# A hybrid decoder layer on one core: earlier fetch of attention's results, two gates moved back, the last inverse from smaller blocks, and tiles shifted by 64 bytes

## The chip, the cores and the metric

The kernel runs on one core of a Trainium2 chip. The metric is the device time of one execution in microseconds; three executions of the kernel before are given, and a profiled one beside them. All numbers of the profile come from that one execution. Its engines are called as the profile calls them: PE (TensorE, matmuls), PEld (the weight loads of TensorE), DVE (VectorE), ACT (ScalarE), POOL (GpSimd) and SP (SyncE, which issues the DMAs).

## The reference, cut to what matters

One layer works on x of 512 tokens by 1024 channels, in float32:

```python
h = rms_norm(x, norm1_w) * (1 + sc1) + sh1
proj = h @ w_in                     # attention q, k, v | RWKV r, k, v and low-rank inputs | 2 x 1024 gates
y_att = attention_mixer(att_in) @ w_att_out
y_rwkv = rwkv7_mixer(rwkv_in, ...) @ w_rwkv_out
g_att, g_rwkv = split(sigmoid(gate_in + b_gate))
x = x + gt1 * ((g_att * y_att + g_rwkv * y_rwkv) @ w_o)
h = rms_norm(x, norm2_w) * (1 + sc2) + sh2
x = x + gt2 * conv_ffn(h, w_up, conv_w, conv_b, w_down)
out = rms_norm(x, norm_f_w)
```

The RWKV mixer carries a 64 by 64 state in each of 16 heads over the 512 tokens:

```python
state = state * w_t + sa * bb_t + v_t * k_t     # sa = state @ aa_t
y_t = state @ r_t
```

## The kernel before, in words

**Products in two halves.** Every large float32 matrix is split into a rounded high part and the rest (`split_w`, `weights`), and a product is three matmuls: high by high, high by low, low by high. ScalarE makes the high part, VectorE the low one. Raw weights come by DMA into a tile with the tag `raw` (two buffers in the pool `wp`), their halves go to `whi` and `wlo` (two buffers each), and a matmul has 128 rows, 128 columns of weights and 512 moving columns.

**The RWKV part by chunks.** The 512 tokens are cut into 8 chunks of 64. The 16 heads make 8 pairs, and two pairs make a group: 4 groups, numbered 0 to 3. For a pair (`pair`, line 1223 on) the projections k, r and v are made, then decays, the products within a chunk (`gram`, tile `gt`) and transposed operands. For a group (`inverse`, line 1436 on) the triangular 64 by 64 matrices of its 32 heads and chunks are inverted at once. Then `chain` (line 1572 on) goes through the 8 chunks in order, each with a few small matmuls that depend on the chunk before, and it ends with a norm over each head (`norm`), transposes (`ty`, into the PSUM tile `t`), and the multiplication with the group's gates.

**The inverse.** A 64 by 64 block is taken as two 32 by 32 diagonal blocks and one below them. `blocks` copies the diagonal blocks out of `gt` (ScalarE), `turned` transposes them so that VectorE works on 32 partitions' worth of blocks side by side, `scaled` multiplies by the reciprocal norms. The recurrence runs from row 30 down to 0 on VectorE: `two(j)` does two rows with a product (L1512), a sum (L1514) and a correction (L1515); `step(j)` does one of the last three rows (L1504, L1505). `rows` and `rows11` transpose back (L1521, L1526), and TensorE makes the block below the diagonal in two visits, `first_pe` and `second_pe`, which write a PSUM tile with the tag `t`. This tag has one buffer; the group's gate product and the transposes at a chain's end use it too.

**The order of the work.** In the RWKV part each instruction is a task of a planner (`Plan`): engine, estimated time, priority, what it waits for, and what it takes and gives back of counted rooms (a buffer of a tile). The planner simulates the engines with these estimates and writes out one order for each engine. The chip keeps that order: an instruction that waits holds all that come behind it on its engine, and the same holds for the DMA queue on SP. Chains and inverses come first; projections of later pairs, of the 16 branch gates (`early_gate`) and of the attention output (`att_out`) fill TensorE with the lowest priority, in the order in which they are created.

**Gates and the attention product.** The 16 gate projections (8 for attention, m = 0 to 7, and 8 for RWKV) have no place in SBUF while pairs are built. `early_gate(m)` makes one, applies tanh (ScalarE, L1816) and stores it in DRAM. When all tasks that are marked `pre` have ended, the sixteen stores among them, the pairs' pool is closed (`close_pre`, t0); `gates` then loads the first eight gates into the pool `pp2`. When the chains of groups 0 and 2 have ended too (`close_even`, t1), the buffers of the even groups are closed, and then `att_out` runs: it loads attention's results in four parts of 256 KB (`load_part`, tag `ld`), splits each into `ahi` and `alo`, and makes 8 blocks of the attention product (`pa`, 12 matmuls each), each multiplied by its gate. `rwkv_ahead` loads and splits the RWKV results of the first groups (`yhi`, `ylo`) and begins three blocks of the RWKV output product (`pr`) as far as groups 0 to 2 reach. Behind the planned part `early_gates` loads the gates 8 to 15, and `rwkv_out`, `mix_out` (product `o` with W_o), `ffn_first`, `ffn_up` (`u`) and `ffn_down` (`o` again) follow.

**Places in SBUF.** Pools on the left are stacked from the bottom, pools on the right from the top. On the left, from below: `cp` (constants), `wp` (weights), then the stage's own, such as `hp` (h's halves `hhi`, `hlo`), `rp`, `cw`, `gp1`, `ip`, `gp0`, later `wo`, `mp` and `fp`. On the right: `pp` (the pairs), later `pp2`, `attp`, `yp`, then `x1p`, `hp2` (`h2hi`, `h2lo`), `uw` (weights of one block of the up projection) and `op`.

Of the kernel before, what the change touches and what calls it, by code (L numbers as in the profile page):

```python
# [10 lines left out]
F32 = mybir.dt.float32  # L11
F32R = mybir.dt.float32r
AF = mybir.ActivationFunctionType
ALU = mybir.AluOpType
# [114 lines left out]
class Layer:  # L129
# [72 lines left out]
    def consts(self):  # L202
# [17 lines left out]
        self.sel2 = cp.tile([P, 2], F32, name="sel2")  # L220
# [820 lines left out]
    def rwkv(self, tail):  # L1041
# [17 lines left out]
        def half():  # L1059

            self.half = self.ip.tile([P, 2], F32, name="half")
            nc.vector.tensor_reduce(self.half, self.ident.rearrange("p (q s y) -> p s q y", q=4, s=2), axis=AX.XY,
                                    op=ALU.add)
# [26 lines left out]
        self.att_out(t1)  # L1090
# [480 lines left out]

    def chain(self, g):
# [132 lines left out]
        for i in range(2):  # L1705
# [43 lines left out]
            t = pe(1.05, gate, [t, self.sgs], S_, take=("t",), give=("g2",), name="gg")  # L1749
            gt_ = sca(0.6, gate_out, [t], E_, take=("gg",), give=("t",))  # L1750
# [32 lines left out]
    def norm(self, yts, t, deps, T_):  # L1783
# [9 lines left out]
        def var():  # L1793
            d["var"] = cw.tile([P, 4], F32, tag="var", name=self.n("var"))
            nc.vector.tensor_reduce(d["var"], d["sq"], axis=AX.X, op=ALU.add)

        def scale():
            rs = cw.tile([P, 4], F32, tag="rs", name=self.n("rs"))
# [19 lines left out]
    def gates(self, opened):  # L1818
# [10 lines left out]
    def early_gates(self, pool):  # L1829
        self.tr_ = [pool.tile([P, S], F32, name=f"gate{m}", tag=f"gate{m}") for m in range(KD, 2 * KD)]  # L1830
# [16 lines left out]
    def open_late(self, pool, lp):  # L1847

        self.lp = lp
        self.ahi, self.alo = [pool.tile([P, 4, S], F32R, name=x, tag=x) for x in ("ahi", "alo")]  # L1850
        self.yhi, self.ylo = [lp.tile([P, KD, S], F32R, name=x, tag=x) for x in ("yhi", "ylo")]

    def att_out(self, opened):

        nc = self.nc
        parts = [self.load_part(lambda k=k: self.att_d[:, k, :], lambda k=k: self.ahi[:, k, :],
# [348 lines left out]
```

## Time and profile before

| | |
|---|---|
| three executions | 1234.45 us median, 1233.17 to 1236.06 |
| the profiled execution | 1231.72 us, span 1230.0 us |
| mean granted PE clock | 0.984 |
| DMA | 139.41 MB, 113 GB/s over the span |
| group 3's recurrence on DVE, first to last operation | 670.83 to 695.99 us |
| the last early gate's matmul on PE begins | 683.22 us |
| group 3's chain on PE begins | 708.29 us |
| last matmul of group 3's chain begins | 754.85 us |
| the up projection's last stretch and the down projection | 858 to 1103 us, 1106 to 1220 us |

The stage that the change touches lies between 655 and 780 us. The stretches before (attention, the first groups) and behind (from 780 on) keep PE busy throughout, but for some short waits.

How to read the views: a row of the timeline has its start and its length in us, the engine, the line, the operation, the tiles (written tile, arrow, read tiles), the shape, the count, and in brackets the idle time of the engine before it with what ended it. Nearly all matmuls have the line L148, a helper; they are told apart by their tiles: `pg<-hhi,whi` a gate, `pa` the attention product, `pr` the RWKV product, `u<-h2hi` the up projection, `u<-cen,v`, `xy`, `xo` and `u<-xs` a chain, `pe` the inverse's visits, `t<-ident,yt` the transposes behind a chain. A matmul's length is modelled and overlaps the next; how often they start is the measure of their pace. The view of stretches has, for each stretch, its length, the busy time of each engine with the count of instructions that touch it, the granted PE clock (1.00 is full), the share of the DMA engines and GB/s.

### The profile page before, as it was taken

The numbers are of one execution on the slowest core, as the hardware profiler recorded it, in microseconds if no ns is written. First come the engines' busy times: TensorE is split into PE (matmuls) and PEld (weight loads), VectorE is DVE, ScalarE is ACT, GpSimd is POOL, SyncE is SP. The second block draws the span as 40 slices with busy tenths as digits, with TensorE's granted clock in tenths as the row PEclk, the third lists the DMA queues.
The fourth block names the chain that finished last, engine by engine and source line by source line (L and its number), as shares of the span: only waits on it lengthen the run. The fifth ranks groups of instructions, "written<-read, shape, count | busy, mean of one in ns | idle before, by whom it ended". The sixth has DMA issues, their size and how long they took to land.

```text
span 1230.0 us, 18481 instructions
## 1 busy us (share of the span) xinstructions
PE 1179.3 (96%) x7200; PEld 946.1 (77%) x7200; DVE 750.2 (61%) x1266; ACT 542.4 (44%) x1011; POOL 109.2 (9%) x228
## 2 busy tenths in 40 slices
PE   4999999999999999999999599999999999999997
PEld 3788887889778776767786467788888888878886
DVE  5687862431668977846896844764556556652135
ACT  4374521522565474465545443444444444442123
POOL 4000000000000013132103122014000000000001
PEclk9899999999999999999999799999999999999999
DMA  9845872120233342413241525460232323233331
GB/s 316 249 132 166 273 229 66 45 80 18 69 103 94 90 112 74 126 47 98 80 114 43 163 58 178 156 206 18 69 103 86 103 86 102 86 103 103 103 120 68
DMA packets 168902, 139.41 MB, mean 113 GB/s; under 512 B 8849, under 2 KB 150251, under 8 KB 168815
## 3 DMA queue, kind: packets, MB, share of 16 engines
q1 hardware_dynamic: 168671, 137.98, 37.0%
q8 instruction: 56, 0.92, 0.3%
q14 instruction: 31, 0.25, 0.1%
q10 hardware_dynamic: 144, 0.26, 0.1%
HBM read 127.65 MB, written 10.56 MB: 112 GB/s over the span
## 4 chain that ended last, share of the span: by engine, by line
PE 79%; DVE 11%; DMA 6%; ACT 2%; issue 2%; SPq 0%; POOL 0%; POOLq 0%; DVEq 0%; ACTq 0%
PE u L148 22%; PE o L148 13%; PE v L148 7%; PE pg L148 7%; PE qk L148 5%; DMA araw<-in_w_ada_dram 4%; PE k L148 3%; PE r L148 2%; PE pa L148 2%; PE pr L148 2%; PE early L148 2%; PE po L148 2%; PE xy L148 2%; PE pt L151 1%; DVE tt L1514 1%
## 5 line engine op out<-in xcount | busy, mean ns | idle before, releaser
L194 DVE TENSOR_TENSOR wlo<-raw,whi 128x1024 fp32r<-128x1024 f32 x65 | 79.7, 1225 | 146.7 <-ACT whi L193 146.6
L148 PE MATMUL u<-h2lo,whi 128*128 128x512 f32 (+2 forms) x368 | 142.3, 387 | 0.0
L148 PE MATMUL u<-h2hi,whi 128*128 128x512 f32 (+2 forms) x368 | 142.3, 387 | 0.0
L148 PE MATMUL u<-h2hi,wlo 128*128 128x512 f32 (+2 forms) x368 | 142.2, 386 | 0.0
L1136 ACT CAST whi<-raw 128x1024 fp32r<-128x1024 f32 (+2 forms) x73 | 72.5, 994 | 123.7 <-PE qk L148 49.5
L193 ACT CAST whi<-raw 128x1024 fp32r<-128x1024 f32 x65 | 68.2, 1049 | 106.5 <-PE o L148 53.7
L1139 DVE TENSOR_TENSOR wlo<-raw,whi 128x1024 fp32r<-128x1024 f32 (+2 forms) x73 | 83.7, 1149 | 19.1 <-ACT whi L1136 18.8
L148 PEld LDWEIGHTS u<-h2lo,whi 128*128 128x128 f32 x368 | 68.9, 187 | 16.0 <-POOL h2lo L405 0.2
L148 PEld LDWEIGHTS u<-h2hi,wlo 128*128 128x128 f32 x368 | 68.9, 187 | 15.5
L148 PEld LDWEIGHTS u<-h2hi,whi 128*128 128x128 f32 x368 | 68.9, 187 | 15.4
L2028 DVE SCALAR_TENSOR_TENSOR u<-u,cols,u 128x511 f32<-128x511 f32 x88 | 65.7, 747 | 4.3 <-ACT u L2026 2.7
L148 PE MATMUL qk<-hhi,wlo 128*128 128x512 f32 x160 | 64.0, 400 | 0.0
L148 PE MATMUL qk<-hlo,whi 128*128 128x512 f32 x160 | 63.6, 397 | 0.0
L148 PE MATMUL qk<-hhi,whi 128*128 128x512 f32 x160 | 63.5, 397 | 0.0
L148 PE MATMUL o<-whi,fhi 128*128 128x512 f32 x144 | 56.1, 390 | 0.3 <-DVE u L2028 0.3
L148 PE MATMUL o<-wlo,fhi 128*128 128x512 f32 x144 | 56.0, 389 | 0.0
L148 PE MATMUL o<-whi,flo 128*128 128x512 f32 x144 | 56.0, 389 | 0.0
L148 PE MATMUL pg<-hhi,wlo 128*128 128x512 f32 x128 | 51.8, 405 | 0.0
L148 PE MATMUL pg<-hlo,whi 128*128 128x512 f32 x128 | 51.7, 404 | 0.0
L148 PE MATMUL pg<-hhi,whi 128*128 128x512 f32 x128 | 51.7, 404 | 0.0
L810 DVE CUSTOM_DVE_ANT_0 sm<-sc,m 128x256 f32<-128x256 f32 (+1 forms) x64 | 23.9, 404 | 37.6 <-PE sc L148 36.5
L347 DVE SCALAR_TENSOR_TENSOR acc<-araw,cols,acc 128x1024 f32<-128x1024 f32 x28 | 35.8, 1280 | 17.2 <-DMA araw<-in_w_ada_dram 17.1
(414 smaller groups left out, 2778.3 us busy)
## 6 DMA issues: line engine op xcount, KB each, us to landing
raw<-in_w_in_dram SPq DMA_DIRECT2D x62, 512.0 KB
raw<-in_w_up_dram SPq DMA_DIRECT2D x44, 512.0 KB
araw<-in_w_ada_dram SPq DMA_DIRECT2D x32, 512.0 KB
raw<-in_w_down_dram SPq DMA_DIRECT2D x22, 512.0 KB
araw<-in_w_ada_dram SPq DMA_DIRECT2D x32, 256.0 KB
wvraw<-in_w_in_dram SPq DMA_DIRECT2D x20, 256.0 KB
gate_d<-gs SPq DMA_DIRECT2D x16, 256.0 KB
gate<-gate_d SPq DMA_DIRECT2D x16, 256.0 KB
```

The costliest lines, as they stand in the source:

```text
L148: return self.nc.tensor.matmul(out, lhsT, rhs, start=start, stop=stop)
L151: self.nc.tensor.matmul(out, in_, self.ident[: in_.shape[0], : in_.shape[0]], is_transpose=True, start=start, stop=stop,)
L193: self.nc.scalar.copy(hl[0], raw)
L194: (lo_eng or self.nc.vector).tensor_tensor(hl[1], raw, hl[0], op=ALU.subtract)
L347: nc.vector.scalar_tensor_tensor(d["acc"], raw, ck, d["acc"], op0=ALU.mult, op1=ALU.add)
L810: nc.vector.tensor_tensor_reduce(d["sm", h][:, :wd], d["sc"][h][:, :wd], m[:, 256 - wd : 256] if gi == 0 else m[:, :wd], 1.0, 3.0e38, op0= ...
L1136: nc.scalar.copy(d["w"][0], d["raw"])
L1139: nc.vector.tensor_tensor(d["w"][1], d["raw"], d["w"][0], op=ALU.subtract)
L1514: nc.vector.tensor_reduce(t[:, n0:, j - 1 : j + 1], x, axis=AX.X, op=ALU.add)
L2028: nc.vector.scalar_tensor_tensor(u[:, d:], pu[:, : S - d], ch(c), u[:, d:], op0=ALU.mult, op1=ALU.add)
```

## The change

- *Late gates.* The gates m = 6 and 7 are no longer early ones. They are projected behind the other fourteen, and their tanh goes straight into `pp2` when the pairs' pool is closed; they are neither stored nor loaded. The close of the pairs' pool (t0) waits for fourteen stores.
- *Attention's results* are fetched at t0 instead of t1, in two loads of 512 KB into the weights' `raw` tiles instead of four of 256 KB into `ld` tiles. `ahi` and `alo` are eight tiles in a pool opened with `pp2`; the gates 8 to 15 are loaded later into these same tiles.
- *The last inverse* (group 3) is made by `inverse16`: the recurrence runs over 16 by 16 blocks, and TensorE joins them into 32 by 32 blocks in two more visits (`half_pe`), each followed by a copy out of PSUM (`half_out`). The other groups keep `inverse`.
- *Rooms.* A group's gate product takes its room `gg` at the matmul and not at the copy behind it.
- *Places.* Small constants share one tile, `var` and `rs` share one, `ss2` has four buffers; the pools above move by 64 or 128 bytes.

```diff
-        self.ones = cp.tile([P, 1], F32, name="ones")
+        few = cp.tile([P, 8], F32, name="few")
+        self.ones, self.mhalf, self.sel2, self.half = few[:, 0:1], few[:, 1:2], few[:, 2:4], few[:, 4:6]
...
-        self.mhalf = cp.tile([P, 1], F32, name="mhalf")
...
-        self.sel2 = cp.tile([P, 2], F32, name="sel2")
...
-            self.inverse(g)
+            (self.inverse16 if g in (3,) else self.inverse)(g)
             self.chain(g)
+        self.late = range(6, KD)
         for m in range(2 * KD):
-            self.early_gate(m)
+            if m not in self.late:
+                self.early_gate(m)
...
         self.gates(t0)
-        self.att_out(t1)
+        self.att_out(t0)
...
+    def inverse16(self, g):
...
+        a0, a1 = [lambda s=s: self.half[:, s : s + 1] for s in range(2)]
+        part = lambda t, c, n: d[t][:, c : c + 16 * n].rearrange("p (y n) -> p y n", n=n)
...
+        def turned():
+            nc.vector.transpose(d["lt"][:, :512].rearrange("p (j i) -> p i j", i=16),
+                                part("lr", 0, 32).rearrange("p y (a i) -> p i a y", a=2))
+
+        def scaled():
+            t = d["lt"][:, :512].rearrange("p (j i) -> p j i", i=16)
+            l = d["l"] = part("lt", 512, 16)
+            nc.vector.scalar_tensor_tensor(l, t[:, :16], a0(), t[:, 16:], op0=ALU.mult, op1=ALU.add)
+            nc.vector.tensor_tensor(l, l, d["rn"][:, :16].unsqueeze(2).to_broadcast([P, 16, 16]), op=ALU.mult)
...
+        def two(j):
+
+            sh = [P, 16 - j, 2, 16 - j]
...
+        def wide0():
+            nc.vector.tensor_scalar(part("lt", 0, 32)[:, :, :16], d["t"], a0(), 0.0, op0=ALU.mult, op1=ALU.add)
+
+        def wide1():
+            nc.scalar.activation(part("lt", 0, 32)[:, :, 16:], d["t"], AF.Copy, scale=a1())
...
+        def half_pe(j):
+
+            if j == 0:
+                d["pe"] = self.cps.tile([P, 512], F32, tag="t", name=self.n("pe"))
+            for y in range(16):
+                for e, b, x in quads:
+                    r = slice(x, x + 32)
+                    l, t = (part("lr", 512, 32)[r, y], d["tc"][r, y, 16:]) if j else (blk(e, b, b)[:, y], d["t11"][r, y, :16])
+                    self.mm(d["pe"][r, 256 * j + 16 * y : 256 * j + 16 * y + 16], l, t, y == 0, y == 15)
...
+        for j in range(14, 2, -2):
+            t = dve(0.55 + 2 * (16 - j) ** 2 / 480, lambda j=j: two(j), [t], name=f"inv{g}")
+        for j in range(2, -1, -1):
+            t = dve(0.37 + (16 - j) ** 2 / 480, lambda j=j: step(j), [t], name=f"inv{g}")
+        t = [dve(0.27, wide0, [t], E_), sca(0.42, wide1, [t], E_)]
+        tc = dve(1.1, rows, t, E_)
+        t = dve(0.72, rows11, [tc], E_)
+        for j in range(2):
+            t = pl.add("PE", 2.6, lambda j=j: half_pe(j), [t, ey], 0.5, take=() if j else ("t",), name="pe")
+            tc = t = sca(0.42, lambda j=j: half_out(j), [t], 0.5, name="pe")
+        t11 = dve(0.72, rows11, [tc], 0.5)
...
-            t = pe(1.05, gate, [t, self.sgs], S_, take=("t",), give=("g2",), name="gg")
-            gt_ = sca(0.6, gate_out, [t], E_, take=("gg",), give=("t",))
+            t = pe(1.05, gate, [t, self.sgs], S_, take=("t", "gg"), give=("g2",), name="gg")
+            gt_ = sca(0.6, gate_out, [t], E_, give=("t",))
...
-            d["var"] = cw.tile([P, 4], F32, tag="var", name=self.n("var"))
+
+            vr = cw.tile([P, 8], F32, tag="var", name=self.n("var"))
+            d["var"], d["rs"] = vr[:, :4], vr[:, 4:]
...
+        def here(m, d):
+            self.p[m] = self.pp2.tile([P, S], F32, name=f"gate{m}", tag=f"gate{m}")
+            self.gate(m, self.p[m], d["pm"])
         for m in range(KD):
-            self.pt[m] = self.pl.add("DMA", 0.8, lambda m=m: load(m), [opened, self.gdt[m]], M_, lag=2.0, name="gate in")
...
+            if m in self.late:
+                t, d = self.body("gate", self.gate_w(m), KD, "mm", lambda: self.mmp("pg"), self.hT)
+                self.pt[m] = self.pl.add("ACT", 0.7, lambda m=m, d=d: here(m, d), [t, opened], E_, give=("mm",))
+            else:
+                self.pt[m] = self.pl.add("DMA", 0.8, lambda m=m: load(m), [opened, self.gdt[m]], M_, lag=2.0, name="gate in")
...
+    def open_att(self, pool):
+
+        self.attp = pool
+        self.ahi, self.alo = [[pool.tile([P, S], F32R, name=f"a{x}{k}", tag=f"gate{KD + 4 * x + k}") for k in range(4)]
+                              for x in range(2)]
...
+    def att_parts(self, q, opened):
+
+        nc, pl = self.nc, self.pl
+        d = {}
+
+        def load():
+            d["t"] = self.wp.tile([P, D], F32, tag="raw", name=self.n("raw"), bufs=2).rearrange("p (k s) -> p k s", k=2)
+            nc.sync.dma_start(d["t"], self.att_d[:, 2 * q : 2 * q + 2, :])
+        t = [pl.add("DMA", 1.6, load, [opened], W_ + 0.01 * q, take=("raw",), lag=2.0)]
...
-            ss, sofar = op.tile([P, 3], F32, name=self.n("ss"), tag="ss2"), None
+            ss, sofar = op.tile([P, 3], F32, name=self.n("ss"), tag="ss2", bufs=4), None
```

More of the change, by code (lines that the diff above doesn't have):

```diff
@@ L1059, in half @@
         def half():
-            self.half = self.ip.tile([P, 2], F32, name="half")
             nc.vector.tensor_reduce(self.half, self.ident.rearrange("p (q s y) -> p s q y", q=4, s=2), axis=AX.XY,
+                                    op=ALU.add)
+            self.eye = self.ip.tile([P, 16], F32, name="eye")
+            nc.vector.tensor_reduce(self.eye, self.ident.rearrange("p (q s y) -> p s y q", q=4, s=2)[:, 1], axis=AX.X,
                                     op=ALU.add)
@@ L2137, in tail @@
             L.pp2 = right.enter_context(pool("pp2", side="right"))
-            def more():
-                yp = right.enter_context(pool("yp", side="right"))
-                L.open_late(att.enter_context(pool("attp", side="right")), yp)
-            return more
+            L.open_att(right.enter_context(pool("attp", side="right")))
+            return lambda: L.open_late(right.enter_context(pool("yp", side="right")))
         L.rwkv(tail)
         att.close()
-        L.early_gates(right.enter_context(pool("gtp", side="right")))
+        L.early_gates()
         L.rw_ctx.close()
```

117 lines of the change are left out of this document (109 added, 8 removed).

## The prediction

> **What bounds the kernel now.** I read the page's totals first, then the busy time by stretch, then the timelines of the one stretch that stood out.
>
> ```profile
> span 1230.0 us, 18481 instructions
> ...
> PE 1179.3 (96%) x7200; PEld 946.1 (77%) x7200; DVE 750.2 (61%) x1266; ACT 542.4 (44%) x1011; POOL 109.2 (9%) x228
> ```
>
> TensorE is busy for 1179 of 1230 us, so a change pays in two ways only: by filling TensorE's gaps, or by making its matmuls shorter. The view of stretches shows where the gaps are (columns: stretch, its length, then PE, PEld, DVE, ACT and POOL busy, the granted clock, the DMA share, GB/s):
>
> ```profile
> 657.00:683.00 26.00, 25.95 (x247) 17.25 (x247) 17.74 (x51) 12.79 (x35) 10.05 (x19) 1.00 0.15 53
> 683.00:690.00 7.00, 4.14 (x59) 2.76 (x58) 6.72 (x14) 2.48 (x8) 2.55 (x3) 0.94 0.66 215
> 690.00:700.00 10.00, 2.90 (x15) 1.72 (x13) 9.64 (x18) 5.36 (x10) 2.17 (x3) 0.50 0.64 193
> 700.00:713.00 13.00, 8.54 (x151) 6.82 (x152) 8.41 (x15) 6.41 (x14) 0.00 (x0) 0.50 0.56 156
> 713.00:756.00 43.00, 43.00 (x414) 28.59 (x413) 17.47 (x36) 18.58 (x54) 10.34 (x21) 1.00 0.24 70
> 756.00:771.00 15.00, 15.00 (x70) 12.00 (x69) 9.63 (x14) 4.62 (x7) 2.89 (x3) 1.00 0.79 246
> 771.00:780.00 9.00, 7.64 (x31) 5.30 (x30) 7.73 (x10) 4.04 (x5) 0.00 (x0) 1.00 0.49 160
> ```
>
> Between 683 and 713 us TensorE works little and at half clock from 690 on. Busy time weighted by the clock is 4.14 x 0.94 + 2.90 x 0.50 + 8.54 x 0.50 = 9.6 us of full-clock work in 30 us: 20.4 us are lost. From 713 to 771 it is full. VectorE is the busy one in the gap (9.64 of 10 us): it runs the last group's inverse.
>
> ```profile
> 664.56 2.04 DVE L1473 STREAM_TRANSPOSE lt<-ld 128x1024 f32<-128x1024 f32 x1 [0.20 <-ACT ld L1469]
> 666.63 1.23 DVE L1478 TENSOR_TENSOR lt<-lt,rn 128x1024 f32<-128x1024 f32 x1
> ```
>
> The blocks are turned and scaled; then comes the recurrence, whose first three and last operation are
>
> ```profile
> 670.83 0.17 DVE L1512 TENSOR_TENSOR tt<-tt,lt 128x4 f32<-128x4 f32 x1
> 671.03 0.16 DVE L1514 TENSOR_REDUCE tt<-tt 128x2 f32<-128x4 f32 x1
> 671.23 0.22 DVE L1515 SCALAR_TENSOR_TENSOR tt<-tt,sup 128x1 f32<-128x1 f32 x1
> ...
> 695.30 0.69 DVE L1505 TENSOR_REDUCE tt<-tt 128x16 f32<-128x512 f32 x1
> 696.02 1.05 DVE L1521 STREAM_TRANSPOSE tt<-tt 128x512 f32<-128x512 f32 x1
> ```
>
> Two transposes turn the result (one is the row above), and TensorE goes on:
>
> ```profile
> 697.66 0.69 DVE L1526 STREAM_TRANSPOSE lt<-tt 128x512 f32<-128x512 f32 x1
> ```
>
> ```profile
> 637.70 1.20 PE L148 MATMUL pe<-lt,gt 32*32 32x32 f32 x64 [0.19 <-DVE lt L1526]
> ...
> 695.79 0.48 PE L151 MATMUL t<-ident,yt 128*128 128x128 f32 x1 [4.45 <-POOL yt L1801]
> ...
> 700.03 1.92 PE L148 MATMUL pe<-lt,gt 32*32 32x32 f32 x64 [1.06 <-DVE y L1765]
> ...
> 708.29 1.12 PE L148 MATMUL u<-cen,v 128*64 128x128 f32 x8 [3.03 <-DVE u L1589]
> ...
> 770.74 0.40 PE L148 MATMUL pr<-yhi,whi 128*128 128x512 f32 x1
> ```
>
> So the order of the gap is: recurrence on VectorE to 696.0, two transposes, two visits to TensorE (pe), then group 3's chain, whose first matmuls stand at 708.29. The matmul at 770.74 is the first that needs group 3's results; its operands are ready when this row ends, at 766.9:
>
> ```profile
> 765.43 1.46 DVE L1875 TENSOR_TENSOR ylo<-y,yhi 128x512 fp32r<-128x512 f32 x2
> ```
>
> **The inverse of 16x16 blocks.** A product or a sum over n elements takes 0.155 + n/960 us (0.17 at 4, 0.69 at 512, rows above), the third step of a pair 0.22, and 0.03 lies between two. Before: 14 pairs with n = 4, 16, 36 ... 784 (4,060 in all) and three single steps (450, 465, 512) make 2 x 5,487/960 + 34 x 0.155 + 14 x 0.22 + 48 x 0.03 = 21.2 us. After: six pairs with n = 8, 32, 72, 128, 200, 288 and three steps with 182, 210, 240 make 2 x 1,360/960 + 18 x 0.155 + 6 x 0.22 + 24 x 0.03 = 7.7. That saves 13.5 us. The first transpose has 512 elements instead of 1,024: 2.04 becomes about 1.05. Scaling becomes two operations over 256 (0.42 each) instead of 1.23. Two more small ones make the norms, +0.4. Together -1.0.
>
> Added behind the recurrence: two copies side by side 0.45, one more transpose 0.69, two copies out of PSUM (256 elements, estimated with the same formula) 0.84, and two visits of 64 matmuls. A visit of 32 matmuls shows as 64 records and takes 1.20 at full clock; twice as many with half the columns lie between 1.2 (if columns or the four independent blocks count) and 2.4. I take 2.4, since these records follow each other by 1.20/64 = 19 ns and look like issue, not columns. Six hops between engines at 0.2 (as the 0.19 and 0.20 in the rows) make 1.2. Sum +8.0. The inverse is shorter by 13.5 + 1.0 - 8.0 = 6.5 us.
>
> Two more things go in the gap. The visit at 700.03 waited behind group 2's transposes, 1.5 us after its operand was ready at 698.35; and two visits at 1.92 become 1.20 if TensorE stays at full clock, 1.4. Group 3's chain then starts 9.4 us earlier, at about 699.
>
> **Late gates and the early fetch.** Who fills TensorE meanwhile? Today the close of the pairs' buffers waits for all sixteen gates. The fourteenth leaves ScalarE with this row
>
> ```profile
> 661.48 0.68 ACT L1816 ACTIVATE gs<-pg,b_gate 128x512 f32<-128x512 f32 x1
> ```
>
> and the last with this one:
>
> ```profile
> 683.76 0.69 ACT L1816 ACTIVATE gs<-pg,b_gate 128x512 f32<-128x512 f32 x1 [0.53 <-PE pg L148]
> ```
>
> With two gates taken out of that condition it falls 22 us earlier, soon after 662, and attention's results are fetched then, in two transfers through the weights' two raw buffers. What queues behind: on SP the six gate loads and the weights of the attention product, which need those buffers; on VectorE four subtractions ahead of the recurrence, in a stretch where it has 17.74 of 26 us in use. The late gates' 48 matmuls still fill TensorE to 683, so some 20 us hide fetch and splitting. From 683 the attention product's 96 matmuls (96 x 0.233 = 22 us, the spacing as below), which today start after 709, fill the gap. The two late gates cost nothing in TensorE time; they save two stores and two loads of 256 KB, off the path.
>
> TensorE's own bound: the matmul at 770.74 comes 20.4 earlier by the loss regained, 4.8 later by the new visits, and 1.0 earlier by the addresses below: 16.6. The chain's bound: results at 766.9 - 9.4, that is 757.5, 13.2 before 770.74; its first half clocked 5 us (708 to 713) may give back 1 to 2 more. The chain is the later one. I take **14.0 us**; its ends are 16.6 and 7, half, should waits take the rest (first rival).
>
> At nothing stand the merged small tiles, the wider spacing of the last stage's sums, and group gates that take their second buffer one step sooner: no instruction is added. The loads of the second eight gates reuse attention's buffers; they wait for the end of pa as today, which comes sooner.
>
> Then 771 to 780 has 1.36 us of idle time, most of it here:
>
> ```profile
> 776.12 1.20 PE L148 MATMUL o<-wohi,mhi 128*128 128x512 f32 x4 [1.03 <-ACT wohi L1808]
> ```
>
> W_o's weights come behind those of the products before it in the same raw buffers, and these are fetched earlier now; I take 0.7 of 0 to 1.4.
>
> **The addresses.** Left-hand pools start at fixed bytes and round tiles up to 32. Today the weights' pool starts at 21,792 = 85 x 256 + 32 and with it everything on the left (weights, hhi, mhi, fhi); the right-hand h2hi, yhi and ahi lie at 224 modulo 256. Three small constants merged into one tile take 64 bytes out: 21,728 = 84 x 256 + 224. All are alike then. Does it matter? These rows say yes (merged chain first: start, length, count; then two stretches with PE's columns alone; then two with all):
>
> ```profile
> 780.66 28.00 PE pr L148 x120
> 808.65 15.67 PE o L148 x69
> ```
>
> ```profile
> 851.31:854.49 3.18, 3.18 (x19) 1.00 0.13 44
> 858.31:861.08 2.77, 2.77 (x17) 1.00 0.00 0
> ```
>
> ```profile
> 900.00:1000.00 100.00, 100.00 (x430) 80.17 (x429) 59.92 (x72) 42.37 (x54) 0.00 (x0) 1.00 0.32 93
> 1110.00:1200.00 90.00, 90.00 (x399) 74.55 (x398) 23.53 (x20) 19.92 (x19) 0.00 (x0) 1.00 0.33 106
> ```
>
> Weights at 32 against yhi at 224: 28.00/120 = 233 ns a matmul. Both at 32 (o): 15.67/69 = 227, next to it and with the same engines at work. Up projection, 32 against 224: (100 + 0.39)/430 = 233.5, a matmul of 0.39 us being counted when it touches the stretch. Down projection, both at 32: 90.39/399 = 226.5. The pair at 851 and 858 is the best witness: both are up projection at 384 columns; the first has its weights on the left (32), the second in a pool on the right (224), like h2hi. Eighteen starts take 3.18 us, 176.7 ns; sixteen take 2.77, 173.1. So a likeness at 224 is as good as one at 32, and it is the likeness that counts.
>
> The up projection has 21 x 2 x 24 = 1,008 matmuls of 512 columns: at 6.4 ns 6.5 us. Its ends are 3.6 (the witness's 3.6 ns) and 7.1 (7.0 ns). The 120 of pr give 0.7. The attention product's 96 and the 54 of pr ahead of 770 are the 1.0 above. VectorE can follow: 59.92 of 100 us are in use there.
>
> The Trainium skill, SBUF — State Buffer, "Who interferes with whom", says that TensorE reads moving operands and weights through two independent ports and never waits for anyone. By that rule the addresses are worth nothing. The trace disagrees: 233.5 against 226.5 ns.
>
> **Sum.** 14.0 + 0.7 + 6.5 + 0.7 = 21.9 us. The profiled execution took 1231.72 us, 1.7 beside its span, and would become 1209.8. It lies 2.7 below the median of 1234.45, from which 1212.5 follows. I forecast **1212.5**.
>
> **Rivals.** *The inverse is caught behind group 2's transposes.* The PSUM buffer t is single; today group 2's transposes take it first, and TensorE stands for 4.45 us with the buffer in hand (row at 695.79). For it: the new inverse needs t longer, over four visits. If the transposes still come first, the first new visit starts at 700.0, and 11 to 12 us (two visits 4.8, copies 0.8, a transpose 0.7, two visits 2.4, copies 1.4, hops 1.4) put group 3's chain at 711.5, 3 us later than today. The fill then only moves work; the stage gives 0 to 2. Time: 1234.45 - 7.9 + 0 = 1226.5. Against it: the new inverse asks for t near 686, nine microseconds before the transposes' last operand. Chance 0.13, with half of that cost as likely as all.
>
> *The addresses are worth nothing,* another cause making pr and u slow: 1234.45 - 14.7 = 1219.8 (TensorE's bound falls to 15.6, still behind the chain's). Against it stands the witness. Chance 0.10. The skill's rule of two ports, named above, would have it so.
>
> *Lying at 224 is itself slow, and the change makes it general* (slower). If each operand at 224 costs the time, not the unlikeness, then u pays for one today and for two after, and the left-hand matmuls now at 227 (by the groups by line: qk 480, gates 384, pairs' k, r, v 576, o and down projection 730, together 2,170) pay for both. That is 2 x 2,170 + 1,008 = 5,350 prices. From 14.7/5,350 = 2.7 ns on it outweighs the stage's gain; at 6.4 ns the time is 1234.45 - 14.7 + 34.2 = 1254. For it: u and pr, the slow ones, do have an operand at 224. Against it: the second row of the witness has two, and is the faster. Chance 0.03.
>
> **How the numbers follow.** The forecast's case has 0.70, the rivals 0.13, 0.10 and 0.03; 0.04 is for what I do not see, mostly small gains. For the range: best ends 16.6 + 1.4 + 7.1 + 0.8 = 25.9, and 2.4 more if a new visit costs 1.2, give 1206; upwards it takes in the case of the addresses and half of the first rival, 1222. The likeliest case's own range is 1207 to 1218. A measurement here tells about 0.2%, 2.5 us, from no change. Faster than that 0.94, within it 0.03, slower 0.03.
>
> **What would show it.** Right: TensorE's clock at 1.00 between 683 and 713 with pa matmuls there; the recurrence on VectorE under 12 us with its neighbours; u<-cen,v of the last group near 699; u at 227 ns, 430 matmuls in 98 us. Wrong: TensorE idle ahead of the new pe visits for more than 2 us each; group 2's transposes ahead of them; a clock of 0.50 later, near 750, because the filling work ran out; u still at 233 ns, or qk and gates above 227. What would make the forecast wrong most: the filling work placed before waits that come late.

## The result and the profile after

The changed kernel takes 1214.14 us (median of 4 runs, 1211.63 to 1217.04); the kernel before, run beside it, 1233.81 us. The ratio is 0.9849, with a 95% interval of 0.9822 to 0.9877: 18.6 us less, where 21.9 were forecast; by the interval it is 15.2 to 22.0. The profiled execution took 1212.94 us. The page's first lines:

```profile
span 1211.2 us, 18982 instructions
...
PE 1170.6 (97%) x7456; PEld 945.9 (78%) x7456; DVE 737.5 (61%) x1248; ACT 542.3 (45%) x1014; POOL 108.6 (9%) x228
```

The view of stretches, for the same times as before the change (the kernel is shifted by 14 us behind the stage, so the last two rows stand beside later work):

```profile
657.00:683.00 26.00, 26.00 (x249) 17.32 (x249) 18.29 (x54) 15.64 (x40) 9.97 (x19) 1.00 0.52 170
683.00:690.00 7.00, 6.51 (x275) 4.92 (x279) 3.29 (x6) 2.73 (x9) 1.82 (x3) 1.00 0.14 40
690.00:700.00 10.00, 7.81 (x196) 5.96 (x186) 2.69 (x4) 5.14 (x11) 0.00 (x0) 0.83 0.19 56
700.00:713.00 13.00, 12.75 (x143) 8.97 (x135) 10.51 (x22) 7.43 (x19) 2.56 (x5) 1.00 0.37 112
713.00:756.00 43.00, 43.00 (x370) 29.69 (x367) 19.62 (x38) 17.34 (x47) 12.65 (x22) 1.00 0.43 132
756.00:771.00 15.00, 15.00 (x67) 12.35 (x66) 12.90 (x19) 7.54 (x10) 0.00 (x0) 1.00 0.40 125
771.00:780.00 9.00, 6.87 (x22) 4.86 (x21) 6.02 (x7) 3.96 (x5) 0.00 (x0) 0.81 0.57 171
```

The gap of 683 to 713 is nearly filled. At full clock TensorE does 6.51 + 7.81 x 0.83 + 12.75 = 25.7 us of work in these 30 us; before it did 9.6. Two smaller losses are new: 690 to 700, and 771 to 780.

The timeline of TensorE through the stage shows the first one:

```profile
686.31 1.26 PE L148 MATMUL pe<-lr,gt 32*32 32x16 f32 x128
689.17 1.26 PE L148 MATMUL pe<-lt,lr 32*32 32x16 f32 x128 [0.48 <-issue]
692.62 0.45 PE L148 MATMUL u<-xs,gt 64*64 64x64 f32 x8 [2.19 <-issue]
...
695.85 1.53 PE L148 MATMUL pe<-lr,gt 32*32 32x32 f32 x64
...
702.84 0.66 PE L148 MATMUL u<-cen,v 128*64 128x128 f32 x8 [0.25 <-DVE u L1762]
...
756.89 0.40 PE L148 MATMUL pr<-yhi,whi 128*128 128x512 f32 x1
```

The two half visits (`half_pe`, 16 columns) take 1.26 us each; the two full ones behind them (`first_pe`, `second_pe`, 32 columns) are the visits that the old inverse has too. Behind the second TensorE stands for 2.19 us, and "issue" says that the trace shows nothing it waited for. Group 3's chain starts at 702.84, 5.5 us earlier than before. The matmul that needs its results, at 770.74 before, stands at 756.89: 13.85 us earlier. VectorE on the same path:

```profile
668.60 0.15 DVE L1656 TENSOR_TENSOR lr<-lt 128x8 f32<-128x8 f32 x1
...
681.98 0.40 DVE L1650 TENSOR_REDUCE lt<-lr 128x15 f32<-128x240 f32 x1
...
690.94 0.71 DVE L1677 STREAM_TRANSPOSE lr<-lt 128x512 f32<-128x512 f32 x1 [4.03 <-ACT lt L1692]
...
755.95 1.46 DVE L2078 TENSOR_TENSOR ylo<-y,yhi 128x512 fp32r<-128x512 f32 x2
```

The recurrence runs from 668.60 to 682.38, 13.8 us with its neighbours; the last transpose ends at 691.65, and the visit that needs it stands at 695.85, because TensorE takes its instructions in order and group 2's and pa's stand ahead. The results are ready when the last row ends, at 757.4, 9.5 us earlier than before, and just when TensorE arrives there: the matmul at 756.89 reads the part that is ready by then.

The second loss, on TensorE and on ScalarE:

```profile
773.70 0.50 PE L148 MATMUL pr<-yhi,whi 128*128 128x512 f32 x1 [1.60 <-ACT whi L193]
774.96 0.62 PE L148 MATMUL pr<-yhi,wlo 128*128 128x512 f32 x1 [0.53 <-DVE wlo L194]
```

```profile
754.89 0.62 ACT L2077 CAST yhi<-y 128x512 fp32r<-128x512 f32 x1 [7.04 <-DVE y L1916]
...
756.59 1.99 ACT L1983 CAST w<-raw 128x1024 fp32r<-128x1024 f32 x2
```

ScalarE stands for 7 us ahead of the cast of group 3's results. Behind it, in order, are the casts of the two weight blocks in the raw buffers, and behind those VectorE's two subtractions (from 759.08 on), which free the buffers. SP issues no weight load between 745.39 and 760.32, and at 772 a block of the RWKV product is late.

The up projection, 100 us of it:

```profile
880.00:980.00 100.00, 100.00 (x443) 82.81 (x442) 61.25 (x75) 43.26 (x56) 0.00 (x0) 1.00 0.34 100
```

100.39/443 = 226.6 ns a matmul, where it was 233.5. By marks in the two traces, the span's 18.8 us are: 13.85 at the first matmul on group 3's results, 1.9 given back by the first up product (851.3 before, 839.4 after), 6.7 won from there to the first down product (1101.8, not 1106 as in the table ahead of the prediction, and 1083.2), and 0.2 at the end.

### The profile page after: what moved, and what is told of

Read it like the earlier page. It is cut to its first block, busy times and chain, and to the rows that moved or that the text cites. A ratio compares the mean times of both kernels' runs of the same rounds, so it can differ in the third digit from the quotient of the medians.

```text
span 1211.2 us, 18982 instructions
## 1 busy us (share of the span) xinstructions
PE 1170.6 (97%) x7456; PEld 945.9 (78%) x7456; DVE 737.5 (61%) x1248; ACT 542.3 (45%) x1014; POOL 108.6 (9%) x228
## 4 chain that ended last, share of the span: by engine, by line
PE 81%; DVE 8%; DMA 6%; ACT 2%; issue 2%; SPq 0%; POOL 0%; POOLq 0%; DVEq 0%; ACTq 0%
PE u L148 22%; PE o L148 13%; PE v L148 7%; PE pg L148 7%; PE qk L148 6%; PE r L148 3%; DMA araw<-in_w_ada_dram 3%; PE k L148 3%; PE pa L148 2%; PE early L148 2%; PE po L148 2%; PE xy L148 2%; PE pr L148 2%; PE xo L148 2%; PE pt L151 1%
```

## The experiments

My theory after the result: the addresses give 6.7 us by the likeness of TensorE's two operands; the stage gives the rest because inverse and filling work go together; and TensorE's own work and group 3's chain now end at the same moment, so that speeding up either alone gives nothing. The rivals: something else made the up products faster; the filling work or the inverse gives the gain by itself; one of the two bounds decides alone; the 2.19 us are an operand's wait. Ratios are to the kernel before, run on the same chip; 0.001 is 1.23 us.

### The addresses

**Back to 32** (x_addr).

```diff
-        few = cp.tile([P, 8], F32, name="few")
+        few = cp.tile([P, 24], F32, name="few")
...
-            self.eye = self.ip.tile([P, 16], F32, name="eye")
+            self.eye = self.few[:, 8:24]
```

> The changed kernel with its left-hand tiles put back by 64 bytes, to 32 modulo 256; the right-hand ones stay at 224, and nothing else moves. If the unlikeness of the addresses costs the time: up products start 233 ns apart again instead of 227, the up projection lasts 243.9 us instead of 237.2, and with pr's 0.7 the kernel takes 1214.1 + 7.4 = 1221.5 us. If another part of the change made these matmuls faster: spacing stays at 227 and the time at 1214.

Measured: 1219.38 us, ratio 0.9896 (0.9877 to 0.9915). The stretch of the up projection:

```profile
890.00:990.00 100.00, 100.00 (x430) 80.17 (x429) 59.86 (x72) 42.27 (x54) 0.00 (x0) 1.00 0.32 94
```

430 again, 233.5 ns, and 6.7 us more from the first up product to the first down product. The spacing of qk, gates and the down projection stays at 227 in both kernels.

**The addresses alone on the kernel before** (b_addr), with the wider spacing of the last stage's sums.

```diff
-        self.ones = cp.tile([P, 1], F32, name="ones")
+        few = cp.tile([P, 8], F32, name="few")
+        self.ones, self.mhalf, self.sel2 = few[:, 0:1], few[:, 1:2], few[:, 2:4]
...
-            ss, sofar = op.tile([P, 3], F32, name=self.n("ss"), tag="ss2"), None
+            ss, sofar = op.tile([P, 3], F32, name=self.n("ss"), tag="ss2", bufs=4), None
```

> The kernel before with the addresses alone changed: three small constants merged into one tile and the last stage's sums spaced as in the changed kernel, so that the left-hand wide tiles lie at 224 modulo 256 like the right-hand ones. If the parts add up: up products 227 ns apart, and 6.5 to 8.5 us less than before, 1224 to 1226 where before takes 1232. If the addresses only pay together with the rest: less than 3 us.

Measured: 1223.48 us, ratio 0.9937 (0.9915 to 0.9958), which is 7.8 us less than before; up products 227 ns apart. This part adds up by itself.

**The matmul alone, all places, and runs of small products** (x_bench). Behind the kernel's end, 24 wide products for each pair of places (p: weights, q: moving operand, in steps of 32 bytes; both start from the same place modulo 256), and then the runs of small ones. The kernel's own time has no meaning here.

```python
a, b = 128 * (i % 8) + 8 * p, 512 * (3 * i % 8) + 8 * q
L.mm(o, W[:, a : a + P], X[:, b : b + 512], i == 0, i == n - 1)
...
r, y = slice(32 * (i % 4), 32 * (i % 4) + 32), i // 4 % 16
L.mm(o[r, c * y : c * y + c], t32[r, :32], t32[r, c * y : c * y + c], True, True)
```

> The changed kernel with measurements behind its end, which use none of its data: first, products of 128x128 weights and 128x512 moving columns, 24 in a row for each of 8 x 8 places of the two operands modulo 256 bytes, with every other engine idle. If likeness modulo 256 decides: 227 ns on the diagonal of the table, about 233 off it, whatever the place itself. If one place is slow by itself: one row or column of the table is. If only other engines' traffic makes the difference: 227 everywhere. Then runs of 16 to 256 products of 32x32 blocks, each followed by 32 wide ones: if TensorE's idle time behind the two half visits (2.2 us) comes from its own instruction supply, idle time shows up behind or within the runs from some length on, though nothing is waited for; if it was a wait that the trace doesn't show, there is none.

Mean spacing in ns of the 20 inner products of each pair, from the trace (four of the eight rows; the others are these, shifted, within 0.8):

```
p\q    0     1     2     3     4     5     6     7
0   226.7 233.5 228.8 233.7 233.3 234.0 233.3 233.2
1   233.2 227.2 233.5 228.8 233.7 233.3 234.0 233.3
4   233.3 234.0 233.3 233.2 227.2 233.4 228.9 233.7
7   233.3 228.9 233.7 233.3 234.0 233.3 233.2 227.2
```

No row and no column is slow: only the difference counts, modulo 256. With every other engine idle, alike places take 227, a moving operand 64 bytes ahead 228.8, all others 232.5 to 234.4. That the two reads collide would explain it; the table shows the difference in place alone. Before the change the up projection's moving operand was 192 ahead, at 233.3.

### The stage

**The old inverse with all the rest** (x_inv).

```diff
-            (self.inverse16 if g in (3,) else self.inverse)(g)
+            (self.inverse16 if g in () else self.inverse)(g)
```

> The changed kernel with the old inverse of 32x32 blocks for the last group. If TensorE's bound and the chain's bound now lie at the same place: the recurrence is 13.5 us longer, the two half visits, their copies and the queue ahead of the first full visit (in all 7 to 12 us) are gone, group 3's chain starts 3 to 7 us later than 702.84, PE stays busy with pa to about 705, and the time is 1214.1 + 3 to 7, about 1219. If the filling work alone gave the gain: the two visits (2.5 us) and the 2.2 us of idle time behind them are saved and the time is 1210 to 1214.

Measured: 1230.81 us, ratio 0.9988 (0.9975 to 1.0001). Neither was right: all but 1.5 us of the whole gain is gone, the addresses' 7.8 included. VectorE shows why; first operation, a stretch near the end, and the transpose behind the last:

```profile
669.29 0.15 DVE L1517 TENSOR_TENSOR tt<-tt,lt 128x4 f32<-128x4 f32 x1
...
707.70 0.25 DVE L1520 SCALAR_TENSOR_TENSOR tt<-tt,sup 128x14 f32<-128x14 f32 x1
707.86 0.68 DVE L2064 SCALAR_TENSOR_TENSOR gate<-gate,pa 128x512 f32<-128x512 f32 x1
708.46 1.22 DVE L1144 TENSOR_TENSOR wlo<-raw,whi 128x1024 fp32r<-128x1024 f32 x1
709.60 0.68 DVE L2064 SCALAR_TENSOR_TENSOR gate<-gate,pa 128x512 f32<-128x512 f32 x1
...
715.60 1.13 DVE L1526 STREAM_TRANSPOSE tt<-tt 128x512 f32<-128x512 f32 x1
```

TensorE's filling work needs VectorE: weights are split for it, its products are multiplied by the gates. The planner ranks all this ahead of the inverse on VectorE (the smaller number goes first: 1 for the products, 2 and a running count for the splits, over 200 for the inverse's steps). That chains and inverses come first, as said ahead of the prediction, holds for TensorE and not here. So a recurrence that took 25.2 us before took 46. Group 3's chain started at 722.6; its results came at 773.1, and TensorE had run out of work by then (busy for 8.19 of the 15 us from 756 to 771).

**The same, with the old inverse's steps ranked first on VectorE** (x_inv_first).

```diff
-        I = I_ + (0.1, 0.2, 0.5, 0.6)[g]
+        I = 0.5 if g == 3 else I_ + (0.1, 0.2, 0.5, 0.6)[g]
```

> The changed kernel with the old inverse of 32x32 blocks for the last group, whose VectorE steps now rank ahead of the filling work's weight splits and products (in the earlier run with the old inverse these lay between its steps, and a recurrence of 21.2 us took 46). If the shared VectorE was the cost there: the recurrence takes 22 to 25 us, the chain starts near 705, and the time is 1217 to 1222. If VectorE's total work is the cost, whoever goes first: the splits come late instead, TensorE runs out of pa matmuls for 5 us or more, and the time is 1225 or above.

Measured: 1221.16 us, ratio 0.9907 (0.9882 to 0.9932), and the recurrence takes 23.5 us. So the shared engine was the cost. But now the filling work waits for VectorE:

```profile
683.00:690.00 7.00, 4.29 (x54) 2.82 (x54) 6.26 (x13) 2.05 (x7) 1.16 (x2) 0.90 0.00 0
690.00:700.00 10.00, 4.20 (x86) 3.36 (x84) 9.42 (x15) 5.15 (x11) 0.00 (x0) 0.50 0.25 76
```

```profile
696.73 1.25 DVE L2052 TENSOR_TENSOR a<-raw,a 128x512 fp32r<-128x512 f32 x2
```

ScalarE had cast attention's results by 676.1; the first two of VectorE's four subtractions for them came at 696.73, behind the whole recurrence. With a long inverse one of the two must wait. That is what the short one is for.

**The short inverse without filling work** (x_alone).

```diff
-        self.late = range(6, KD)
+        self.late = range(KD, KD)
...
-        self.att_out(t0)
+        self.att_out(t1)
```

> The changed kernel without its filling work: all sixteen gates early, attention's results fetched only when the chain of the even groups has closed its buffers, as before the change. The short inverse and the addresses stay. If the short inverse pays by itself: group 3's chain starts as early as in the changed kernel (near 700), but TensorE stands or runs at half clock between 683 and 700 and loses 8 to 12 us there, so the time lies at 1222 to 1226. If only both together pay (the chain is early, yet TensorE's own bound stays where it was): 1226 to 1229, the addresses' 6 to 8 us being all that is left.

Measured: 1219.91 us, ratio 0.9900 (0.9878 to 0.9922). The chain is earliest of all so far (first matmuls at 695.3, results at 753.6), yet TensorE is at half clock:

```profile
683.00:690.00 7.00, 4.96 (x184) 4.11 (x175) 1.23 (x3) 3.71 (x8) 0.00 (x0) 0.70 0.80 260
690.00:700.00 10.00, 8.05 (x126) 6.26 (x120) 2.08 (x4) 4.19 (x12) 1.82 (x3) 0.50 0.64 214
```

From b_addr (0.9937), the short inverse alone gives 0.0037 (4.6 us), the filling work alone costs 0.0051 (6.3 us) in the planner's ranks, and both together give 0.0088 (10.9 us). With the old inverse ranked first (x_inv_first) the filling work gives 0.0030 (3.7 us) instead, not clear of nothing; so the loss of 6.3 belongs to the ranks and not to the filling work itself. The differences of two ratios are uncertain by 0.0025 to 0.0035.

**All gates early, attention fetched early** (x_gates): the first of those two edits alone.

```diff
-        self.late = range(6, KD)
+        self.late = range(KD, KD)
```

> The changed kernel with all sixteen gates early again (attention's results are still fetched as soon as the pairs' buffers close). If the early close is what lets the filling work run: the last gate holds the close to about 683, the fetch and the split take until about 691, PE is idle or at half clock for 6 to 9 us there, and the time is 1220 to 1223. If the two gates only change places with other work and the chain is the bound: 1213 to 1216.

Measured: 1218.70 us, ratio 0.9892 (0.9874 to 0.991), 5.3 us above the changed kernel (uncertain by some 4); pa started at 704.2 instead of 681.3, and the clock was 0.50 from 690 to 700. The two late gates are what lets the fetch come early; without them nothing can be told between this run and x_alone (0.9892 and 0.9900).

**The short inverse ranked first on VectorE** (x_first), in the new function:

```diff
-        I = I_ + (0.1, 0.2, 0.5, 0.6)[g]
+        I = 0.5
```

> The changed kernel with the short inverse's VectorE steps ahead of the filling work's (the recurrence now takes 13.8 us with its neighbours, 7.7 by itself). If the chain sets the end of this stage: its results come some 5 us earlier and the time is 1209 to 1211. If TensorE's own work sets it by now (the first matmul on group 3's results stood at 756.9 without idle time before it): the results wait, and the time is 1213 to 1215.

Measured: 1213.01 us, ratio 0.9836 (0.9811 to 0.9862), not told apart from the changed kernel, though the results came at 752.1. The matmul on them stands at 755.47, without a wait: TensorE's own work sets it. The profiled execution, 1208.26 us, was the fastest of four; the others took 1212.17 to 1214.20. By its trace it is 4.7 us below the changed kernel's, 1.4 at this matmul and 3.3 behind it, where the loss at 771 is absent.

**The half visits split** (x_split):

```diff
-            for y in range(16):
+            for y in range(8 * h, 8 * h + 8):
...
-            t = pl.add("PE", 2.6, lambda j=j: half_pe(j), [t, ey], 0.5, take=() if j else ("t",), name="pe")
+            t = pl.add("PE", 0.65, lambda j=j: half_pe(j, 0), [t, ey], 0.5, take=() if j else ("t",), name="pe", lag=1.0)
+            t = pl.add("PE", 0.65, lambda j=j: half_pe(j, 1), [t], 0.5, name="pe")
```

> The changed kernel with each of the two half visits split in two runs of 32 products and wide products of pa placed between them. If TensorE's instruction supply is what stands behind the visits (in the measurement by itself, 2.1 to 2.3 us of idle time came after some 175 to 207 records of 16 columns, and 0.5 where 1.65 us of wide products lay between runs of 128): the 2.2 us shrink to 0.5 or less, TensorE's clock stays at 1.00 between 690 and 700, and the profile's stage from group 2's chain to the first up product is 2 to 4 us shorter; the time is 1210 to 1213. If the idle time was a wait for an operand: it stays, 1213 to 1217.

Measured: 1215.26 us, ratio 0.9861 (0.9842 to 0.988). TensorE:

```profile
691.39 0.53 PE L148 MATMUL pe<-lt,lr 32*32 32x16 f32 x40
692.47 0.38 PE L148 MATMUL pe<-lt,lr 32*32 32x16 f32 x24 [0.55 <-issue]
...
756.51 0.74 PE L148 MATMUL pr<-yhi,whi 128*128 128x512 f32 x2 [2.01 <-ACT yhi L2078]
```

The stall shrank to 0.55 us, and the clock stays at 1.00 from 683 to 713. The time did not follow: TensorE now waits 2 us for the results (the row at 756.51), and the loss at 771 is still there (6.21 of 9 us busy, clock 0.81).

**Both together** (x_both): the edits of x_first and x_split, nothing else.

> The same split, and the short inverse's VectorE steps ahead of the filling work's, as in the earlier run with the inverse first (1213.0). If supply and VectorE's order are both costs: the idle time behind the visits is gone and group 3's results come some 5 us earlier than in the changed kernel; the time is 1207 to 1211. If TensorE's own work sets the end of the stage: no better than the split alone, 1211 to 1214.

Measured: 1204.50 us, ratio 0.9785 (0.9759 to 0.981), by the ratios 7.9 us below the changed kernel (uncertain by some 4.6), and below x_first and x_split too. Set against the 1233.81 us of the first comparison, the ratio gives 1207, the low end of the first case.

```profile
690.00:700.00 10.00, 10.00 (x141) 7.41 (x140) 7.16 (x16) 6.02 (x16) 2.40 (x5) 1.00 0.54 159
...
771.00:780.00 9.00, 9.00 (x41) 7.45 (x40) 7.36 (x9) 4.79 (x6) 0.00 (x0) 1.00 0.50 162
```

```profile
747.73 1.46 DVE L2079 TENSOR_TENSOR ylo<-y,yhi 128x512 fp32r<-128x512 f32 x2
```

Results at 749.2, 8.2 us earlier than in the changed kernel, and the matmul on them at 751.44 without a wait. That matmul is 5.4 us earlier than in the changed kernel: each repair alone uncovered the other bound, and together they pay. The other part of the gain, 3.2 us by the first up product, lies behind it: 15 of W_o's products now stand ahead of pr's rest, as they did before the change, so the loss at 771 is gone too. Single traces of one stage scatter: x_addr and x_order, which leave it as in the changed kernel, have this matmul at 758.8 and 759.0 instead of 756.89.

**What the stall is.** In x_bench nothing is waited for, as everything lies ready. One small product shows as two records in the trace. Runs of 32 to 128 records of 16 columns pass without idle time, and so do 256 records of 32 columns (2.35 us); runs of 192, 256 and 512 records of 16 columns do not. The longest:

```profile
1634.46 1.64 PE L148 MATMUL bt<-b 32*32 32x16 f32 x175
1638.23 1.25 PE L148 MATMUL bt<-b 32*32 32x16 f32 x128 [2.13 <-issue]
1641.70 1.90 PE L148 MATMUL bt<-b 32*32 32x16 f32 x128 [2.22 <-issue]
1645.44 1.30 PE L148 MATMUL bt<-b 32*32 32x16 f32 x81 [1.85 <-issue]
```

The view of DMA from 1632 to 1650 us names the one kind of traffic in that time:

```profile
DMA packets 4, 0.07 MB, mean 4 GB/s; under 512 B 0, under 2 KB 0, under 8 KB 0
## 3 DMA queue, kind: packets, MB, share of 16 engines
q8 instruction: 4, 0.07, 1.4%
```

Four packets of 16 KB with instructions, at 1635.84, 1639.36, 1642.86 and 1646.58, each about 1 us long; each stall ends 1.4 to 1.5 us after the end of one (1.3 to 1.6 for all stalls of this run). The instructions come 16 KB at a time, and in no trace here closer than 3.3 us. In the changed kernel the packets stand at 686.87, 690.28 and 693.75, as close, around the two visits, and its two stretches of idle time, 0.48 and 2.19 us, end 1.4 us after the end of the first and of the second packet. x_split has them 4.3 and 3.7 apart, and its 0.55 us end 1.45 us after one. Where 1.65 us of wide products lay between runs of 128 the stall was 0.5 us. Its price is more than itself: the 32 wide products behind a stall took 9.2 to 10.3 us instead of 7.55, and the granted clock from 1610 to 1621 was 0.71, where it is 1.00 behind the runs that did not stop.

The number of columns is not what lets a run pass. Over four blocks, as here, both kinds have the same pace:

```profile
1589.44 0.73 PE L148 MATMUL bt<-b 32*32 32x16 f32 x64
...
1655.94 0.75 PE L148 MATMUL bt<-b 32*32 32x32 f32 x64
...
1672.81 2.35 PE L148 MATMUL bt<-b 32*32 32x32 f32 x256
```

The last run differs in its packets: one had ended 0.4 us before it began, while for the three runs that stopped the last one had ended 6 to 8 us before. That this decides fits the rows and was not varied by itself.

### The weights at 771

**The two splits on GpSimd** (x_pool).

```diff
-            self.split(raw, *w)
+            nc.gpsimd.tensor_copy(w[0], raw)
+            nc.gpsimd.tensor_tensor(w[1], raw, w[0], op=ALU.subtract)
```

> The changed kernel with the split of the two weight blocks that W_o's weights queue behind (the fourth and fifth of the RWKV output product) done on GpSimd instead of ScalarE and VectorE, so that these splits no longer stand behind the casts of group 3's results, for which ScalarE is idle for 7 us. If that queue starves the two raw buffers: transfers go on between 750 and 760, the 2.4 us of idle time of PE between 771 and 788 and the 1.8 us lost at reduced clock there go away, and the time is about 1211. If the transfers' own pace through two buffers is the limit: the idle time only moves, 1213 to 1215. If GpSimd is too slow for it (the first block is needed at 759.6): PE idles there, up to 1218.

Measured: 1214.08 us, ratio 0.9856 (0.983 to 0.9881). The next loads are issued 3 to 5 us earlier (755.37 and 758.17), but the results come later, at 760.1. VectorE and GpSimd:

```profile
756.32 2.38 DVE L1916 SCALAR_TENSOR_TENSOR y<-y,cols,gg 128x512 f32<-128x512 f32 x1
```

```profile
752.95 5.19 POOL L2113 TENSOR_TENSOR w<-raw,w 128x1024 fp32r<-128x1024 f32 x2
```

The product y takes 2.38 us instead of 0.75, and ends 0.6 us after GpSimd's subtraction. The Trainium skill, SBUF — State Buffer, "SBUF: two separate sides", says that VectorE with two SBUF inputs and a GpSimd operation that reads SBUF share one pair of ports as an exclusive lock: the one that starts first has it for its whole instruction, and the other fully blocks. These rows agree: y could end only once GpSimd's 5.19 us were over.

**Two blocks loaded ahead of W_o's first rows** (x_order).

```diff
-            if 2 < m < KD - 2:
-                ahead.append(block(m + 2))
+            if m in (0, 1, 5):
+                ahead.append(block({0: 5, 1: 6, 5: 7}[m]))
```

> The changed kernel with two of the last three weight blocks of the RWKV output product loaded ahead of W_o's first rows in the two raw buffers (today three rows of W_o, needed only from 793 on, go first). If that order starves TensorE between 771 and 788: the 2.4 us of idle time and the 1.8 us at reduced clock go away, and the time is about 1211. If two buffers are too slow in any order: the idle time comes back ahead of the last block or of W_o's rows, 1213 to 1216.

Measured: 1215.30 us, ratio 0.9858 (0.9833 to 0.9882). The stretch of 771 to 780 is full, and the idle time comes back ahead of the last block:

```profile
788.81 0.50 PE L148 MATMUL pr<-yhi,whi 128*128 128x512 f32 x1 [3.72 <-ACT whi L193]
```

## Why the prediction was right, and where it was not

- **The stage, 14.0 us: 13.85 measured,** from two sides. TensorE's bound: I let all 20.4 us of loss come back; 4.3 stayed (30 less 25.7). The new visits cost 2 x 1.26 = 2.5 us, not 4.8: the lower of my two bounds. 20.4 - 4.3 - 2.5 is 13.6. Of the 1.0 that I gave the addresses here, pa's part did not come: its matmuls stand 233 ns apart before and 232 after. The chain's bound: results at 757.4, as said (757.5).
- **The chain's start at 699 was wrong** (702.84). Inside the inverse the recurrence took 13.8 us with its neighbours, not under 12. The visits were 2.3 us shorter; the stall and the queue on TensorE, in which the first full visit stood for 4.2 us, took more than that back. The chain itself made it up: 54.6 us from first matmul to results, 58.6 before. 2.7 of these 4.0 us lie in its first step, which before ran at half clock and which I had booked as 1 to 2; 1.3 lie behind its last matmul, where before a weight split stood among VectorE's operations.
- **"The chain is the later one" was too sharp.** Both ended within half a microsecond. By their medians x_first and x_split, which each removed one of them, moved nothing that can be told; x_both moved 7.9 us, 5.4 of its trace's 8.4 at this place.
- **What queues on VectorE** was the step that I worked out too little. I named four subtractions ahead of the recurrence. What matters is the splits and products of the filling work between its steps: they made 46 us of the long recurrence, and with it the filling work is a loss of 6.3 us. My sum adds fill and inverse. In the planner's ranks it holds only since both came in one change; with the long inverse ranked first the parts come near it (3.7 and 4.6 against 10.9 together, each uncertain by some 4).
- **771 to 780, 0.7 us of gain, was the step that failed:** 1.9 us were lost from the results to the first up product, where with pr's 0.7 the sum had 1.4 won. These 3.3 us are about what the sum of 21.9 has above the traces' 18.8. Idle time rose from 1.37 to 2.37 us, and nine matmuls behind it ran 0.43 us apart instead of 0.23 (1.8 us). I saw that W_o's weights came late in the raw buffers, and took an earlier stage to mean earlier loads. But the buffers are freed by splits that stand behind the cast of group 3's results, and with the rest earlier, TensorE came to these weights sooner than they did. Its order changed as well: before, 15 of W_o's products (from 776.12 on) stood ahead of pr's last 120, and the weights of the last 72 of these are loaded behind three rows of W_o; in the changed kernel, x_addr, x_split, x_pool and x_order none do. Neither experiment on it won anything; the traces of x_first and x_both, which have W_o's products in front again, show no loss there beyond 0.7 us of idle time.
- **The addresses, 6.5 us: 6.7,** and 227 ns as said. The rule of two independent ports in the Trainium skill (SBUF — State Buffer, "Who interferes with whom") would have given nothing; x_addr, b_addr and the table say that the places of TensorE's two operands do matter to each other, by up to 3% where they differ.
- **The rivals.** The inverse wasn't caught behind group 2's transposes: these came at 703.78, after all four visits. Another cause for the slow up products is refuted by x_addr and b_addr. Lying at 224 is not slow by itself: the table's diagonal is the same at every place, and qk and the gates stayed at 227.
- Of the signs named ahead, two of "wrong" appeared in part: idle time of over 2 us at a new visit (behind it, not ahead), and a lower clock later (0.81, at 771). Of those of "right", three were missed: the recurrence, the chain's start, and the clock, which was 0.83 between 690 and 700.

Left open: why 64 bytes ahead is nearly as good as alike; how long a run of small products may be in a given program (alike in form, one stopped after 175 records and one after 207); and what put W_o's products behind pr's in one order and ahead in the other.

## What to carry to other kernels

A gap in one engine is filled with work that other engines prepare: count what the filling asks of the engine that the gap waits for, and rank the two there on purpose. Where two bounds end at the same moment, repair both before judging either. Look at where the wide operands of TensorE lie: moving one side by 64 bytes was worth 7.8 us of 1232 here.

## What the runs showed of the hardware that was not expected

- A 128x128 by 128x512 product (fp32r) takes 227 ns where weights and moving operand start at the same byte modulo 256, 228.8 where the moving operand is 64 ahead, and about 233.5 elsewhere, with every other engine idle.
- TensorE can outrun its instruction supply: 16 KB packets came at least 3.3 us apart, and 32x32 products of 16 columns (9.4 to 9.8 ns a record) stop for 1.9 to 2.3 us after some 175 to 207 records. 256 records of 32 columns, at 9.2 ns, passed once, right behind a packet.
- In the kernel 64 products of 16 columns took 1.26 us and 32 of 32 columns 1.20 us, but columns don't set the pace: in x_bench 32 products took 0.73 us with 16 columns and 0.75 with 32. The half visits and x_bench go round four 32x32 blocks, the full visits two; that the number of blocks sets the pace fits both, and no run varied it by itself.
